# The hand-written order at the mixer/FFN boundary carried on through the squares of x1; the last norm weight loaded into the place of the up projection's activations

## The chip, the cores and the metric

One core of one Trainium2 chip runs the kernel. The metric is the device time of one execution in microseconds (us), as the median of several runs; a profile is one further execution with its own time.

## What is computed

One decoder layer for 256 tokens of width 2048, all in float32. Cut to what matters here:

```python
x = x + rms_norm(mixed, ln_mix_post)          # mixed = [attention || SSM] @ w_out
h = rms_norm(x, ln_ffn_pre)                   # this x is called x1 below
u = causal_depthwise_conv(h @ w_ffn_up, ffn_conv_w, ffn_conv_b)
gate, up = split(u, [5632])
f = (gelu(gate) * up) @ w_ffn_down
x = x + rms_norm(f, ln_ffn_post)
# rms_norm(x, w) = x * rsqrt(mean(x*x) + 1e-6) * w
```

## The kernel before

**Weights.** Every matrix is read in units of 128 x 1024 float32 (512 KB). SyncE issues the load of a unit into one of 4 `raw` buffers (L71). ScalarE rounds it to float32r, `whi` (L72), VectorE takes the rest, `wlo = raw - whi` (L73), and TensorE multiplies with both. A load can start when the `wlo` of four units before is done, and a cast when TensorE is through with the unit whose `whi` place it takes. From the boundary on there are 4 + 3 places for `whi` and for `wlo` (`ws.deepen`). A unit of the up projection is 8 pairs of products (L202 with `whi`, L203 with `wlo`); a unit of the down projection is 12 products (L265 to L267). `fetch` loads and splits one unit; `fetch_rounded` only loads and casts it and hands back the subtraction for later. `tick` fetches one unit (two, while the deeper buffers fill) and counts down the work that `defer(n, ...)` put off by n units.

**The boundary.** The last chunk of `w_out` ends in an order written by hand for TensorE, ScalarE and VectorE (`tc.manual_schedule`); elsewhere a scheduler orders each engine's instructions. In the written part the two token halves (t = 0, 1) get the factor of the norm behind the mixer (`factor`), x1 times the next norm's weight is formed in four chunks of 512 columns (`scaled`), transposed on TensorE (`turn`, L785), and evacuated as a high part by ScalarE (L787) and a low part by VectorE (`finish`, L790) into `h2`, the activations of the up projection. Three column tiles of the up projection (`held_up`, six units) are multiplied token half by token half as the pieces come (L210, L213).

The rms factor of this second norm is not in `h2`. It is multiplied in later, behind the up projection, by `rb2`, which holds it along tokens. For this, x1 itself is formed in `xt` (`residual`, L778 on VectorE, 8 pieces of which one is done early), each piece is squared and summed on ScalarE (L185, output `junk`), and `second_rms` reduces the sums on VectorE (`sum1`), takes the power on GpSimd (`rsy`, L144) and refines it on VectorE (`rsq`, then `rsr`, L148). Two TensorE transposes (`prb`, L179) and a ScalarE copy (L180) bring it into `rb2`. They are deferred by 5 units:

```python
defer(5, lambda: along_tokens(rb2, [sums[:, t:t + 1] for t in range(NT)]))
defer(60, load_post)
```

**The last norm weight.** `wpo` holds `ln_ffn_post` on all partitions. `load_post` (deferred by 60 units) issues a broadcast load of 1024 KB from GpSimd's queue and multiplies the tile by -0.5 on ScalarE. It is first read when the first column chunk of the second half of the down projection is complete (`fdone`, L939). The FFN runs in two halves: 22 pairs of column tiles of the up projection with convolution and gelu (`gated`) into `gT`, then four chunks of the down projection.

Of the kernel before, what the change touches and what calls it, by code (L numbers as in the profile page):

```python
# [9 lines left out]
F32 = mybir.dt.float32  # L10
# [9 lines left out]
P = 128  # L20
D = 2048
S = 256
NT = S // P
# [23 lines left out]
V_MIXPOST, V_FFNPRE, V_FFNPOST, V_HEADS = 0, D, 2 * D, 3 * D  # L47
# [68 lines left out]
def decoder_layer(ctx, tc, x, xT, win, wdt, wout, wup, wdown, relb, vec, cols, mconv, fconv,  # L116
                  consts, onehot, out):
    nc = tc.nc
    ctx.enter_context(nc.allow_non_contiguous_dma(reason="overlapping rows of the bias table"))

    pers = ctx.enter_context(tc.tile_pool(name="pers", bufs=1))
# [4 lines left out]
    aux = nc.gpsimd.dma_start  # L126

    def row_bcast(off, n):
        return bass.AP(tensor=vec.tensor, offset=vec.offset + off, ap=[[0, P], [1, n]])
# [7 lines left out]
    def chunk(c):  # L137
        return slice(c * 512, (c + 1) * 512)
# [12 lines left out]
    def mean_rsqrt(src, inv):  # L151

        w = src.shape[-1]
        a = pers.tile([P, w], F32, name="rsa", tag=f"rsa{w}", bufs=4)
        nc.vector.tensor_scalar(a, src, inv, EPS, op0=ALU.mult, op1=ALU.add)
        return rsqrt(a)
# [27 lines left out]
    def square_sum(dst, src):  # L184
        nc.scalar.activation(junk, src, AF.Square, accum_out=dst)  # L185
# [37 lines left out]
    def defer(units, fn, *args):  # L223

        pending.append([units, fn, args])

    def tick():
        ws.tick()
        for p in pending:
            p[0] -= 1  # L230
        due = [p for p in pending if p[0] <= 0]
        pending[:] = [p for p in pending if p[0] > 0]
        for _, fn, args in due:
            with tc.issue_after(end[0]):
                fn(*args)
# [56 lines left out]
    def rows_tail(pss, aT, kts, tail, t, j):  # L292
        rows_part(pss[t], tail[j], aT, kts[len(kts) - HOLD + j], t, False, j == HOLD - 1)

    ws = Weights(nc, wp, [win[i] for i in range(win.shape[0])]
                 + [wout[i] for i in range(wout.shape[0])]
                 + [w for half in range(2)
                    for w in [wup[half * 88 + i] for i in range(88)]
                    + [wdown[half * 44 + i] for i in range(44)]])
# [19 lines left out]
    with ExitStack() as mctx:  # L319
# [404 lines left out]
        xt = pers.tile([P, NT, D], F32, name="xt", tag="xt", bufs=1)  # L724
# [16 lines left out]
        ss1 = pers.tile([P, NT, 4], F32, name="ss1")  # L741
# [18 lines left out]
        def factor(t, ps):  # L760

            square_sum(ss[0][t][:, 3:4], ps)
            return late_rsqrt(ss[0][t][:, 3:4], early[t], lambda: nc.vector.tensor_tensor(
                mm[:, t, chunk(3)], ps, wpost[:, chunk(3)], op=ALU.mult))

        def scaled(t, q):

            if (t, q) == (0, 3):
                residual(t, q)
                nc.vector.tensor_tensor(ml[t][q], xt[:, t, chunk(q)], lnrow[:, chunk(q)],  # L770
                                        op=ALU.mult)
            else:
                nc.vector.scalar_tensor_tensor(ml[t][q], ml[t][q], rs[t], xl[t][q], op0=ALU.mult,
                                               op1=ALU.add)

        def residual(t, q):
            x1 = xt[:, t, chunk(q)]
            nc.vector.scalar_tensor_tensor(x1, mm[:, t, chunk(q)], rs[t], x1, op0=ALU.mult,  # L778
                                           op1=ALU.add)

        def turned(t, q):
# [8 lines left out]
                last.append(nc.vector.tensor_tensor(dst[1], pt, f32(dst[0]), op=ALU.subtract).ins)  # L790
            return rest, last

        def second_rms():
            for t in range(NT):
                for q in range(4):
                    if (t, q) != (0, 3):
                        residual(t, q)
                    square_sum(ss1[:, t, q:q + 1], xt[:, t, chunk(q)])
            a = pers.tile([P, NT], F32, name="sum1")
            nc.vector.tensor_reduce(a, ss1, axis=AX.X, op=ALU.add)  # L800
            return mean_rsqrt(a, 1.0 / D)
# [13 lines left out]
        rs, rest, units = [], {}, []  # L815
# [6 lines left out]
        def second_tokens(q):  # L822
            for i, ps in enumerate(held_up):
                for k in range(q * 4, q * 4 + 4):
                    cols_tok(ps, units[k // 8 * 3 + i], h2, k, k % 8, 1)
# [5 lines left out]
        def turn(t, q):  # L831
            rest[t, q] = turned(t, q)

        def finish(t, q):
            rest[t, q][0]()

        E = mybir.EngineType
        with tc.manual_schedule(engines={E.PE, E.Activation, E.DVE}):
            for j in range(HOLD):
                rows_tail(pss, mT, both, tail, 0, j)  # L840
            rs.append(factor(0, pss[0]))
            scaled(0, 0)
            scaled(0, 1)
            scaled(0, 2)
            t1_units(0, 1)
            more = [ws.fetch_rounded()]
            t1_units(1, 2)
            more.append(ws.fetch_rounded())
            t1_units(2, 3)
            turn(0, 0)  # L850
            turn(0, 1)
            finish(0, 0)
            finish(0, 1)
            scaled(0, 3)
            more[0]()
            t1_units(3, 4)
            more.append(ws.fetch_rounded())
            t1_units(4, 5)
            rs.append(factor(1, pss[1]))
            more.append(ws.fetch_rounded())  # L860
            units.extend(ws.take() for _ in range(6))
            turn(0, 2)
            first_tokens(0)
            turn(0, 3)
            scaled(1, 0)
            finish(0, 2)
            first_tokens(1)
            scaled(1, 1)
            finish(0, 3)
            turn(1, 0)  # L870
            first_tokens(2)
            turn(1, 1)
            finish(1, 0)
            more[1]()
            finish(1, 1)
            first_tokens(3)
            scaled(1, 2)
            weighted(1, 3)
            second_tokens(0)
            turn(1, 2)  # L880
            scaled(1, 3)
            more[2]()
            finish(1, 2)
            more[3]()
            second_tokens(1)
            turn(1, 3)
            finish(1, 3)
            second_tokens(2)
            second_tokens(3)
        tick()  # L890
        came = rest[1, 3][1]
        with tc.issue_after(came[0]), tc.issue_after(came[1]):
            for _ in range(5):
                tick()
            sums = second_rms()

    fp = ctx.enter_context(tc.tile_pool(name="fp", bufs=1))
    fcv = fp.tile([P, 2 * NF, 4], F32, name="fcv")
    aux(out=fcv, in_=fconv)
    wpo = fp.tile([P, D], F32, name="wpo")  # L900
    gT = fp.tile([P, HALF, 2, S], F32R, name="gT")
    fa = pers.tile([P, NT, D], F32, name="fa", tag="mm", bufs=1)
    rb2 = pers.tile([P, S], F32, name="rb2", tag="rbc", bufs=1)

    def load_post():
        aux(out=wpo, in_=row_bcast(V_FFNPOST, D))
        nc.scalar.mul(wpo, wpo, -0.5)

    def summed(ps):
        u = fp.tile([P, S], F32, name="cfu", tag="cf", bufs=8)  # L910
# [52 lines left out]
    def gated(i, ug, uu):  # L963
        cg = conv_ffn(i, ug)
        nc.scalar.activation(cg, cg, AF.Gelu_apprx_tanh)
        cu = conv_ffn(NF + i, uu)
        k = i % HALF
        nc.vector.tensor_tensor(cu, cg, cu, op=ALU.mult)
        split_evac(gT, k, slice(0, S), cu)

    held = []
    defer(5, lambda: along_tokens(rb2, [sums[:, t:t + 1] for t in range(NT)]))
    defer(60, load_post)
    for half in range(2):
        for i in range(half * HALF, (half + 1) * HALF):
            ps = held_up[2 * i:2 * i + 2]
            for _ in range(2 - len(ps)):
                ps.append(col_psum())
                cols_tile(ps[-1], h2)
            us = [summed(p) for p in ps]  # L980
            if i < 2:
                defer(5 - 2 * i, gated, i, *us)
            else:
                gated(i, *us)
        for c in range(4):
            if half == 0 and c >= 2:
                held.append([psum("ph") for _ in range(NT)])
                rows_chunk(held[-1], gT, range(0, HALF, 2), last=False)
            elif half == 1 and c == 2:
                rows_chunk(held[0], gT, range(0, HALF, 2), first=False, done=fdone(1, c))  # L990
            elif half == 1 and c == 3:
                fearly += [early_sum(ss[2][t][:, :3]) for t in range(NT)]
                kts = range(0, HALF, 2)
                tail = rows_to_tail(held[1], gT, kts, first=False)
                for t in range(NT):
                    for j in range(HOLD):
                        rows_tail(held[1], gT, kts, tail, t, j)
                    fdone(1, 3)(t, held[1][t])
            else:
                rows_chunk(chunk_psums(), gT, range(0, HALF, 2), done=fdone(half, c))  # L1000
# [105 lines left out]
```

## Time and profile before

| | |
|---|---|
| median of 3 runs | 1142.55 us (1141.38 to 1145.75) |
| the profiled execution | 1141.79 us |
| its span from first to last instruction | 1140.0 us |
| TensorE busy (products) | 1126.8 us, 99% |
| VectorE / ScalarE / GpSimd busy | 788.4 / 592.2 / 12.0 us |
| mean granted TensorE clock | 0.997 of full |

A time in a row below is counted from the start of the span. PE is TensorE, PEld its weight loads, DVE VectorE, ACT ScalarE, POOL GpSimd, SP SyncE; a q behind the name (SPq) is the engine's issue of DMAs. In a timeline a row holds start, duration, engine, line, operation, output<-input, shapes and count, and in brackets how long the engine stood idle before it and what released it.

### The profile page before, as it was taken

Reading aid. Unit: us, or ns where it says so; the run is one execution under the profiler, and the core shown is the slowest. Engines: PE = TensorE matmul, PEld = TensorE weight load, DVE = VectorE, ACT = ScalarE, POOL = GpSimd, SP = SyncE. Lnnn points to the kernel's source line nnn. Section 1 sums busy time; section 2 is a strip of 40 time slices with the busy share of each in tenths; the row PEclk is TensorE's granted clock in tenths of the full one; section 3 lists DMA queues with packets and bytes.
Section 4 is the critical chain, followed back from the end, with each engine's and each line's share of the span. In section 5 each row is a group of like instructions: output and inputs, shape, how many; then the busy total and the mean of one; then the engine's idle time right before and its main releaser. Section 6 shows DMA issues by size and latency. Waiting matters only on the chain.

```text
span 1140.0 us, 15818 instructions
## 1 busy us (share of the span) xinstructions
PE 1126.8 (99%) x5912; PEld 957.3 (84%) x5912; DVE 788.4 (69%) x1268; ACT 592.2 (52%) x913; POOL 12.0 (1%) x22
## 2 busy tenths in 40 slices
PE   9999999999999989999999999999999999999997
PEld 7877888888878978888888888888888888888886
DVE  6587886766667788787877644447878777765552
ACT  6555544554454476555555544335555555554441
POOL 0000000000000000000000000000000000000000
PEclk9999999999999999999999999999999999999999
DMA  8756444555587275565556565566555555655542
GB/s 299 285 169 197 141 158 135 183 169 167 173 328 242 97 272 173 192 189 186 185 186 186 188 196 186 187 194 189 187 185 186 186 187 190 191 188 186 188 161 74
DMA packets 60148, 215.53 MB, mean 189 GB/s; under 512 B 7119, under 2 KB 7800, under 8 KB 59176
## 3 DMA queue, kind: packets, MB, share of 16 engines
q1 hardware_dynamic: 58696, 207.69, 56.3%
q0 software_dynamic: 1088, 6.48, 1.6%
q8 instruction: 46, 0.75, 0.3%
q10 hardware_dynamic: 288, 0.35, 0.1%
q14 instruction: 30, 0.25, 0.1%
HBM read 212.39 MB, written 2.11 MB: 188 GB/s over the span
## 4 chain that ended last, share of the span: by engine, by line
PE 94%; DMA 2%; ACT 1%; DVE 1%; issue 1%; SPq 0%; POOL 0%; POOLq 0%; ACTq 0%
PE pa L202 35%; PE pa L203 18%; PE pa L265 8%; PE pa L266 8%; PE pa L267 8%; PE ph L267 4%; PE ph L266 4%; PE ph L265 4%; PE pab L202 1%; DMA raw<-in_wout_dram 1%; DMA wpo<-in_vec_dram 1%; DVE wlo L73 1%; PE py L568 1%; PE pab L203 1%; ACT whi L72 1%
## 5 line engine op out<-in xcount | busy, mean ns | idle before, releaser
L73 DVE TENSOR_TENSOR wlo<-raw,whi 128x1024 fp32r<-128x1024 f32 (+1 forms) x385 | 469.5, 1222 | 271.1 <-ACT whi L72 262.0
L72 ACT CAST whi<-raw 128x1024 fp32r<-128x1024 f32 (+1 forms) x385 | 402.8, 1047 | 466.1 <-PE pa L202 221.5
L202 PE MATMUL pa<-h,whi 128*128 128x512 f32 x1360 | 479.7, 396 | 0.0
L203 PE MATMUL pa<-h,wlo 128*128 128x256 f32 x1360 | 384.1, 282 | 0.0
L202 PEld LDWEIGHTS pa<-h,whi 128*128 128x128 f32 x1360 | 256.2, 188 | 60.3
L203 PEld LDWEIGHTS pa<-h,wlo 128*128 128x128 f32 x1360 | 256.5, 189 | 0.1
L202 PE MATMUL pa<-hT,whi 128*128 128x512 f32 x384 | 138.5, 399 | 0.0
L203 PE MATMUL pa<-hT,wlo 128*128 128x256 f32 x384 | 108.3, 283 | 0.0
L202 PEld LDWEIGHTS pa<-hT,whi 128*128 128x128 f32 x384 | 72.2, 188 | 16.5 <-issue 0.2
L920 DVE SCALAR_TENSOR_TENSOR cfc<-cfu,fcv,cfc 128x254 f32<-128x254 f32 (+1 forms) x176 | 83.4, 479 | 1.9 <-ACT cfc L918 0.5
L203 PEld LDWEIGHTS pa<-hT,wlo 128*128 128x128 f32 x384 | 72.2, 188 | 0.3 <-issue 0.2
L267 PE MATMUL pa<-whi,gT 128*128 128x512 f32 x176 | 69.4, 394 | 0.0
L267 PE MATMUL ph<-whi,gT 128*128 128x512 f32 x176 | 69.3, 394 | 0.0
L265 PE MATMUL ph<-whi,gT 128*128 128x512 f32 x176 | 69.2, 393 | 0.0
L266 PE MATMUL ph<-wlo,gT 128*128 128x512 f32 x176 | 69.2, 393 | 0.0
L265 PE MATMUL pa<-whi,gT 128*128 128x512 f32 x176 | 69.2, 393 | 0.0
L266 PE MATMUL pa<-wlo,gT 128*128 128x512 f32 x176 | 69.2, 393 | 0.0
L918 ACT ACTIVATE cfc<-cfu,fcv 128x256 f32<-128x256 f32 x88 | 52.3, 599 | 0.6 <-DVE cfu L917 0.6
L265 PE MATMUL pa<-whi,hT 128*128 128x512 f32 x128 | 51.7, 404 | 0.2 <-DVE xsT L219 0.2
L267 PE MATMUL pa<-whi,hT 128*128 128x512 f32 x128 | 50.7, 396 | 0.0
L266 PE MATMUL pa<-wlo,hT 128*128 128x512 f32 x128 | 50.6, 395 | 0.0
L266 PE MATMUL pa<-wlo,mT 128*128 128x512 f32 x128 | 50.2, 392 | 0.3 <-DVE wlo L73 0.3
(238 smaller groups left out, 1148.1 us busy)
## 6 DMA issues: line engine op xcount, KB each, us to landing
raw<-in_wup_dram SPq DMA_DIRECT2D x176, 512.0 KB, 3.6
raw<-in_wdown_dram SPq DMA_DIRECT2D x88, 512.0 KB, 3.5
raw<-in_win_dram SPq DMA_DIRECT2D x87, 512.0 KB, 3.5
raw<-in_wout_dram SPq DMA_DIRECT2D x32, 512.0 KB, 4.2
xsq<-in_x_dram SPq DMA_DIRECT2D x2, 1024.0 KB, 8.0
xt<-in_x_dram POOLq DMA_DIRECT2D x2, 1024.0 KB, 7.0
xr<-in_xT_dram SPq DMA_DIRECT2D x7, 256.0 KB, 6.1
out_dram<-xt SPq DMA_DIRECT2D x6, 256.0 KB, 2.4
```

Of the source, the lines that this page charges most:

```text
L72: nc.scalar.copy(hi[:, s], raw[:, s])
L73: return lambda: nc.vector.tensor_tensor(lo[:, s], raw[:, s], f32(hi[:, s]), op=ALU.subtract)
L202: nc.tensor.matmul(ps, w[0][:, s], aT[:, k, :, :], start=(k == 0), stop=False)
L203: end[0] = nc.tensor.matmul(ps[:, :S], w[1][:, s], aT[:, k, 0, :], start=False, stop=(k == KT - 1)).ins
L265: nc.tensor.matmul(ps, a, w[0][:, s], start=(first and j == 0), stop=False)
L266: nc.tensor.matmul(ps, a, w[1][:, s], start=False, stop=False)
L267: end[0] = nc.tensor.matmul(ps, b, w[0][:, s], start=False, stop=(last and j == 1)).ins
L568: nc.tensor.matmul(py[:, i * 64:(i + 1) * 64], rows[:, t, g, i, :], xcs[t, g][:, i * 64:(i + 1) * 64], start=True, stop=True)
L918: nc.scalar.activation(c, u, AF.Identity, scale=wv[:, 2:3], bias=wv[:, 3:4])
L920: nc.vector.scalar_tensor_tensor(c[:, sh:], u[:, :S - sh], wv[:, 2 - sh:3 - sh], c[:, sh:], op0=ALU.mult, op1=ALU.add)
```

## The change

Two things are edited. First, the written order does not stop behind the last `second_tokens`: the pieces of x1, their squares and four more units of weights (`more[4]` to `more[7]`) are written into it piece by piece, with the square of the chunk that is done early (0, 3) first. The scheduler's part behind it fetches two units instead of six before the sums are reduced. Second, `wpo` no longer has a place of its own. It is allocated behind the up projection of the second half under the tag of `h2`, and loaded and scaled there.

```diff
+        def second_square(t, q):
+            square_sum(ss1[:, t, q:q + 1], xt[:, t, chunk(q)])
+
         def second_rms():
-            for t in range(NT):
-                for q in range(4):
-                    if (t, q) != (0, 3):
-                        residual(t, q)
-                    square_sum(ss1[:, t, q:q + 1], xt[:, t, chunk(q)])
             a = pers.tile([P, NT], F32, name="sum1")
             nc.vector.tensor_reduce(a, ss1, axis=AX.X, op=ALU.add)
             return mean_rsqrt(a, 1.0 / D)
@@ -878,33 +876,44 @@
             weighted(1, 3)
             second_tokens(0)
             turn(1, 2)
+            more.append(ws.fetch_rounded())
             scaled(1, 3)
+            finish(1, 2)
             more[2]()
-            finish(1, 2)
             more[3]()
             second_tokens(1)
             turn(1, 3)
             finish(1, 3)
+            more[4]()
             second_tokens(2)
             second_tokens(3)
-        tick()
-        came = rest[1, 3][1]
-        with tc.issue_after(came[0]), tc.issue_after(came[1]):
-            for _ in range(5):
-                tick()
-            sums = second_rms()
+            second_square(0, 3)
+            more.append(ws.fetch_rounded())
+            for q in range(2):
+                residual(0, q)
+                second_square(0, q)
+            more[5]()
+            more.append(ws.fetch_rounded())
+            residual(0, 2)
+            second_square(0, 2)
+            residual(1, 0)
+            second_square(1, 0)
+            more[6]()
+            more.append(ws.fetch_rounded())
+            for q in range(1, 4):
+                residual(1, q)
+                second_square(1, q)
+            more[7]()
+        for _ in range(2):
+            tick()
+        sums = second_rms()
 
     fp = ctx.enter_context(tc.tile_pool(name="fp", bufs=1))
     fcv = fp.tile([P, 2 * NF, 4], F32, name="fcv")
     aux(out=fcv, in_=fconv)
-    wpo = fp.tile([P, D], F32, name="wpo")
     gT = fp.tile([P, HALF, 2, S], F32R, name="gT")
     fa = pers.tile([P, NT, D], F32, name="fa", tag="mm", bufs=1)
     rb2 = pers.tile([P, S], F32, name="rb2", tag="rbc", bufs=1)
-
-    def load_post():
-        aux(out=wpo, in_=row_bcast(V_FFNPOST, D))
-        nc.scalar.mul(wpo, wpo, -0.5)
 
     def summed(ps):
         u = fp.tile([P, S], F32, name="cfu", tag="cf", bufs=8)
@@ -970,7 +979,6 @@
 
     held = []
     defer(5, lambda: along_tokens(rb2, [sums[:, t:t + 1] for t in range(NT)]))
-    defer(60, load_post)
     for half in range(2):
         for i in range(half * HALF, (half + 1) * HALF):
             ps = held_up[2 * i:2 * i + 2]
@@ -982,6 +990,10 @@
                 defer(5 - 2 * i, gated, i, *us)
             else:
                 gated(i, *us)
+        if half == 1:
+            wpo = pers.tile([P, D], F32, name="wpo", tag="h", bufs=1)
+            aux(out=wpo, in_=row_bcast(V_FFNPOST, D))
+            nc.scalar.mul(wpo, wpo, -0.5)
         for c in range(4):
             if half == 0 and c >= 2:
                 held.append([psum("ph") for _ in range(NT)])
```

**The squares on ScalarE.** The first rows are ScalarE's before, from the scaling of `wpo` on, with the second to the sixth of the eight squares (`junk,ss1_3090<-xt`); whi is a unit's cast, cfu the copy of a finished column tile out of PSUM.

```order
L907 ACTIVATE wpo_3879<-wpo_3879 128x2048
L72 CAST whi_3840<-raw_3839 128x1024
L185 ACTIVATE junk_67,ss1_3090<-xt_3066 128x512
L72 CAST whi_3907<-raw_3906 128x1024
L185 ACTIVATE junk_67,ss1_3090<-xt_3066 128x512
L72 CAST whi_3929<-raw_3928 128x1024
L185 ACTIVATE junk_67,ss1_3090<-xt_3066 128x512
L218 COPY cfu_3934<-pq_3491 128x256
L185 ACTIVATE junk_67,ss1_3090<-xt_3066 128x512
L218 COPY cfu_3937<-pa_3889 128x256
L185 ACTIVATE junk_67,ss1_3090<-xt_3066 128x512
```

The same stretch of ScalarE with the change, from the third square to the cast behind the eighth and last:

```order
L185 ACTIVATE junk_67,ss1_3090<-xt_3066 128x512
L72 CAST whi_3826<-raw_3825 128x1024
L185 ACTIVATE junk_67,ss1_3090<-xt_3066 128x512
L218 COPY cfu_3885<-pa_3490 128x256
L185 ACTIVATE junk_67,ss1_3090<-xt_3066 128x512
L72 CAST whi_3836<-raw_3835 128x1024
L185 ACTIVATE junk_67,ss1_3090<-xt_3066 128x512
L72 CAST whi_3849<-raw_3848 128x1024
L185 ACTIVATE junk_67,ss1_3090<-xt_3066 128x512
L72 CAST whi_3855<-raw_3854 128x1024
L185 ACTIVATE junk_67,ss1_3090<-xt_3066 128x512
L72 CAST whi_3906<-raw_3905 128x1024
```

The scaling of `wpo` is gone from here; a cast and a square or two alternate up to the last square, and the cast of the seventh unit (`whi_3906`) comes behind it. The six units that TensorE takes next are whi_3726, 3816, 3826, 3836, 3849 and 3855 (before: 3810, 3816, 3822, 3828, 3834, 3840).

**The norm's factor on VectorE.** VectorE's rows before, which end with the factor `rsr`:

```order
L73 TENSOR_TENSOR wlo_3930<-raw_3928,whi_3929 128x1024
L219 TENSOR_TENSOR cfu_3934<-pq_3491,cfu_3934 128x256
L219 TENSOR_TENSOR cfu_3937<-pa_3889,cfu_3937 128x256
L73 TENSOR_TENSOR wlo_3959<-raw_3957,whi_3958 128x1024
L73 TENSOR_TENSOR wlo_3981<-raw_3979,whi_3980 128x1024
L800 TENSOR_REDUCE sum1_3860<-ss1_3090 128x2
L155 TENSOR_SCALAR rsa_3862<-sum1_3860 128x2
L145 TENSOR_TENSOR rsq_3865<-rsy_3864 128x2
L73 TENSOR_TENSOR wlo_4004<-raw_4002,whi_4003 128x1024
L146 TENSOR_TENSOR rsq_3865<-rsq_3865,rsa_3862 128x2
L147 TENSOR_SCALAR rsq_3865<-rsq_3865 128x2
L148 TENSOR_TENSOR rsr_3866<-rsy_3864,rsq_3865 128x2
```

With the change:

```order
L73 TENSOR_TENSOR wlo_3856<-raw_3854,whi_3855 128x1024
L798 TENSOR_REDUCE sum1_3860<-ss1_3090 128x2
L219 TENSOR_TENSOR cfu_3882<-pa_3489,cfu_3882 128x256
L155 TENSOR_SCALAR rsa_3862<-sum1_3860 128x2
L219 TENSOR_TENSOR cfu_3885<-pa_3490,cfu_3885 128x256
L145 TENSOR_TENSOR rsq_3865<-rsy_3864 128x2
L73 TENSOR_TENSOR wlo_3907<-raw_3905,whi_3906 128x1024
L146 TENSOR_TENSOR rsq_3865<-rsq_3865,rsa_3862 128x2
L219 TENSOR_TENSOR cfu_3933<-pq_3491,cfu_3933 128x256
L147 TENSOR_SCALAR rsq_3865<-rsq_3865 128x2
L73 TENSOR_TENSOR wlo_3929<-raw_3927,whi_3928 128x1024
L148 TENSOR_TENSOR rsr_3866<-rsy_3864,rsq_3865 128x2
```

Before, three subtractions `wlo` for later units stood ahead of the reduction `sum1` in these rows and one inside the chain; now the reduction comes right behind the sixth unit's `wlo_3856`, and two subtractions (3907, 3929) and three of the sums `cfu` stand between the steps of the chain. On TensorE `prb` has moved up by one pair of products: it stood behind the first pair of the sixth unit (`whi_3840`), now it stands right ahead of that unit (`whi_3855`).

**The scaling of wpo on ScalarE.** ScalarE's rows before at the start of the second half's down projection, where `cfc` and `gT` belong to the last column tiles of the up projection and the whi are units of `w_ffn_down`:

```order
L72 CAST whi_9431<-raw_9430 128x1024
L965 ACTIVATE cfc_9384<-cfc_9384 128x256
L918 ACTIVATE cfc_9390<-cfu_9381,fcv_3877 128x256
L72 CAST whi_9449<-raw_9448 128x1024
L190 CAST gT_3880<-cfc_9390 128x256
L72 CAST whi_9467<-raw_9466 128x1024
```

And with the change:

```order
L72 CAST whi_9431<-raw_9430 128x1024
L974 ACTIVATE cfc_9381<-cfc_9381 128x256
L927 ACTIVATE cfc_9387<-cfu_9378,fcv_3877 128x256
L996 ACTIVATE wpo_9395<-wpo_9395 128x2048
L190 CAST gT_3879<-cfc_9387 128x256
L72 CAST whi_9449<-raw_9448 128x1024
L72 CAST whi_9467<-raw_9466 128x1024
```

The scaling of `wpo`, which waits for its load, now stands ahead of the last `gT` and of all casts of the down projection from `whi_9449` on. On GpSimd's queue the load waits for TensorE's last product with `h2`, and stands behind the power `rsy` instead of ahead of it.

## Rows read from the trace of the kernel before

**Rows 1.** The page: the span, and the busy time of the engines.
```profile
span 1140.0 us, 15818 instructions
...
PE 1126.8 (99%) x5912; PEld 957.3 (84%) x5912; DVE 788.4 (69%) x1268; ACT 592.2 (52%) x913; POOL 12.0 (1%) x22
```

**Rows 2.** Waits on TensorE, whole span: total us, times, longest.
```profile
PE prb L179 <- DVE rsr L148: 4.5, 1, 4.5
```

**Rows 3.** Two stretches: span, busy time by engine, granted clock, DMA share, GB/s.
```profile
402.90:417.30 14.40, 14.40 (x84) 12.47 (x82) 11.07 (x15) 11.73 (x22) 0.00 (x0) 1.00 0.76 279
422.20:426.20 4.00, 4.00 (x16) 3.40 (x15) 4.00 (x10) 2.45 (x5) 0.00 (x0) 0.57 0.77 244
```

**Rows 4.** Timeline of TensorE, from the second tokens to behind the gap.
```profile
399.25 0.28 PE L213 MATMUL pq<-h,wlo 128*128 128x256 f32 x1
...
402.89 0.39 PE L202 MATMUL pa<-h,whi 128*128 128x512 f32 x1
...
416.97 0.39 PE L202 MATMUL pa<-h,whi 128*128 128x512 f32 x1
...
421.99 0.43 PE L179 MATMUL prb<-cst,rsr 128*128 128x128 f32 x2 [4.51 <-DVE rsr L148]
422.17 0.48 PE L202 MATMUL pa<-h,whi 128*128 128x512 f32 x1
...
426.25 0.40 PE L202 MATMUL pa<-h,whi 128*128 128x512 f32 x1
```

**Rows 5.** Timeline of ScalarE around the squares of x1.
```profile
397.46 0.59 ACT L787 CAST h<-pxt 128x512 fp32r<-128x512 f32 x1 [2.62 <-PE pxt L785]
...
404.85 1.05 ACT L72 CAST whi<-raw 128x1024 fp32r<-128x1024 f32 x1 [3.08 <-DMA raw<-in_wup_dram]
...
406.89 1.92 ACT L907 ACTIVATE wpo<-wpo 128x2048 f32<-128x2048 f32 x1 [0.72 <-DMA wpo<-in_vec_dram]
...
409.65 0.62 ACT L185 ACTIVATE junk<-xt 128x512 f32<-128x512 f32 x1
...
410.27 1.03 ACT L72 CAST whi<-raw 128x1024 fp32r<-128x1024 f32 x1
```

**Rows 6.** Timeline of VectorE around the same stretch.
```profile
394.88 0.69 DVE L790 TENSOR_TENSOR h<-pxt,h 128x512 fp32r<-128x512 f32 x1 [0.69 <-ACT h L787]
...
399.35 3.49 DVE L73 TENSOR_TENSOR wlo<-raw,whi 128x1024 fp32r<-128x1024 f32 x3
...
407.07 2.73 DVE L778 SCALAR_TENSOR_TENSOR xt<-mm,lsr,xt 128x512 f32<-128x512 f32 x4
...
412.25 0.75 DVE L219 TENSOR_TENSOR cfu<-pa,cfu 128x256 f32<-128x256 f32 x2
...
419.12 0.17 DVE L155 TENSOR_SCALAR rsa<-sum 128x2 f32<-128x2 f32 x1
...
420.13 0.16 DVE L145 TENSOR_TENSOR rsq<-rsy 128x2 f32<-128x2 f32 x1 [0.84 <-POOL rsy L144]
```

**Rows 7.** DMA issues of three stretches: KB each, median us from issue to landing.
```profile
wpo<-in_vec_dram POOLq DMA_DIRECT2D x1, 1024.0 KB, 8.3
raw<-in_wup_dram SPq DMA_DIRECT2D x1, 512.0 KB, 7.4
...
raw<-in_wup_dram SPq DMA_DIRECT2D x1, 512.0 KB, 4.6
...
lnrow<-in_vec_dram POOLq DMA_DIRECT2D x1, 1024.0 KB, 15.2
```

**Rows 8.** Timeline of ScalarE at the start of the second down projection.
```profile
1015.10 1.05 ACT L72 CAST whi<-raw 128x1024 fp32r<-128x1024 f32 x1 [0.88 <-PE pa L267]
...
1017.89 1.05 ACT L72 CAST whi<-raw 128x1024 fp32r<-128x1024 f32 x1 [1.44 <-PE pa L267]
```

**Rows 9.** TensorE's last product with h2, and VectorE's first reading of wpo.
```profile
1009.25 0.28 PE L203 MATMUL pa<-h,wlo 128*128 128x256 f32 x1
...
1042.31 1.29 DVE L939 TENSOR_TENSOR fa<-fa,wpo 128x512 f32<-128x512 f32 x2
```

## The prediction, as put on record before the run

> **What bounds the kernel now.** I read the page first. TensorE is busy for 1126.8 of 1140.0 us [rows 1]: only time in which TensorE stands still, or runs slowly, can be won. The waits on TensorE come second. By far the longest is 4.5 us, once, of `prb` for the factor `rsr` [rows 2]. The windows around it show a second cost: up to 417.3 TensorE is busy throughout at a granted clock of 1.00, and in the 4.0 us behind the gap the clock is 0.57 [rows 3], a mixture of its two levels, 2.4 and 1.2 GHz; ahead of it the engine had stood still.
>
> The full price is read from TensorE's timeline. From 402.89 to 416.97 it starts 40 pairs of products, 0.352 us a pair [rows 4]. The pair at 416.97 is the first of the sixth unit; without a gap its second would start at 417.32. Seven pairs and the two transposes remain up to the seventh unit: 417.32 + 7 x 0.352 + 0.18 (from the start of `prb` to the next product, 421.99 to 422.17) = 419.96. It starts at 426.25 [rows 4]. So the wait costs **6.3 us**: 4.67 of standing still (421.99 - 417.32) and 1.6 of slow products behind it.
>
> Why is `rsr` late? The sums of the squares are through the first step only at 419.12 [rows 6]. Two things had held ScalarE up before the squares. A cast waited 3.08 us for its raw unit, up to 404.85, and then the scaling of `wpo` waited 0.72 and took 1.92 [rows 5]. Both go back to one transfer: `wpo`'s 1024 KB took 8.3 us (so they were issued near 398.6), and a raw unit issued beside them took 7.4 where one issued as they ended took 4.6 [rows 7].
>
> **The change part by part.** *Nothing is added or dropped.* The same products, casts, squares, loads and sums run; so the sum consists of waits alone.
>
> *1. The squares.* I follow the new order with the durations of the rows. In VectorE's queue a subtraction takes 1.16 (3.49 / 3), a piece of x1 0.68 (2.73 / 4), a sum `cfu` 0.37 (0.75 / 2); on ScalarE a cast takes about 0.95 to 1.05 and a square with its readout 0.62 (409.65 to 410.27) [rows 5, 6]. Up to VectorE's evacuation at 394.88 the two orders are alike. Then VectorE: `wlo_3590` to 396.7, `wlo_3611` to 397.8, the last evacuation from 398.08 (ScalarE's part ends at 398.05 [rows 5]) to 398.7, `wlo_3727` to 399.8, two pieces of x1 to 401.2, `wlo_3817` to 402.3, two pieces to 403.7, `wlo_3827` to 404.8, three pieces to 406.8, then 3837 to 408.0, 3850 to 409.1 and 3856 to 410.3. ScalarE runs beside it and is free from 398.05: square, cast 3816 to 399.6, second square at 400.5, and so on; its eighth square can end at 409.5, ahead of VectorE, if the raw units come in time. Each raw unit is issued when a subtraction four units before ends. Cast 3826 starts at 402.3 and its unit is issued at 396.8; 3836: 404.8 and 397.9; 3849: 406.3 and 399.9; 3855: 407.9 and 402.4. That leaves 5.5, 6.9, 6.4 and 5.5 us. With 4.6 us for a unit nothing waits; with 7.4 each would.
>
> The factor then: reduction 410.3, a `cfu`, `rsa` from 410.8, the step through GpSimd (419.12 to 420.13, 1.01 [rows 6]) to 411.8, `wlo_3907` to 413.1, `rsq` and a `cfu` to 413.8, `wlo_3929` to 415.0, `rsr` to **415.2**. `wlo_3929` needs cast 3928, whose unit is issued at 408.0: with 4.6 us it lands at 412.6 and is cast by 413.7, in time. TensorE comes to `prb` at 416.97, since it now stands ahead of the sixth unit. So there are about 1.8 us to spare, the wait disappears whole, the engine does not stand still and the clock stays up: -6.3 us. Which landing time I take decides: 4.6, because what made 7.4 is the 1024 KB transfer that is no longer there; 7.4 is the bad bound, costed as a rival. What is late next, if anything, is a subtraction: `wlo_3590` now comes behind an evacuation instead of ahead of it, and so 3590 and 3611 end at 396.7 and 397.8. TensorE wants 3611 in the product at 399.25 [rows 4] and 3590 eight products earlier: 1.4 us of room. All later units are ready 3 to 10 us ahead. I cost these moves at nothing; if the cover went, each us late costs a us and, by the gap above, up to 1.6 more in clock.
>
> *2. The load of `wpo`.* It is now issued when TensorE has read `h2` for the last time, 1009.5 in the times of before (1009.25 + 0.28) [rows 9]. With 8.3 us [rows 7] it lands at 1017.8, and ScalarE, which waits for it from 1014.2 on (free since 0.88 before 1015.10 [rows 8]), has scaled it by 1019.8 (1.92). Queued behind it on ScalarE are the last `gT` and every cast of the down projection; behind those casts wait VectorE's subtractions, the raw loads and at last TensorE. The cast at 1015.10 is the first that is held up. It fills one of seven places, just left by TensorE, so it is used six units later; TensorE frees one each 2.79 us [rows 8], so about 1031.8. With 0.40 for `gT`, 1.05 for the cast and 1.22 for the subtraction ScalarE must be through with `wpo` by 1029.1: 9.3 us of room. The casts behind it run at 1.05 each against 2.79 of need and catch up. The slowest broadcast load of this size in the trace, `lnrow` with 15.2 us [rows 7], would still leave 2.4 us. `gT` is read in the eleventh unit, and `wpo` at 1042.31 [rows 9]. So: 0 from both ends; the load costs from 17.6 us on.
>
> The Trainium skill (DMA: Bandwidth & Descriptors, Rules for kernel authors) speaks against this part: issue a load early, compute, and wait for it late, while here the wait stands right behind the issue. By that rule ScalarE pays most of the load, and the rows agree that it would stand idle for some 3.6 us; but by the room just worked out none of it reaches TensorE, and the sum is the same.
>
> **The sum.** 1141.79 (span 1140.0 and 1.79 around it) - 6.3 = 1135.5 for an execution like the profiled one. The profiled one lies 0.76 under the median of the runs, by which it would be 1136.3. I say **1135.9**. A difference of 0.5%, 5.7 us, is about what can be told from no change here; the bound is 1136.8, and my forecast is only just past it.
>
> **The rivals.** *Part of the wait stays.* If raw units keep taking 7.4 us, I get cast 3826 at 404.2, 3855 at 409.9, the reduction at 412.1, cast 3928 at 417 and `rsr` at 419.6 in place of 415.2. TensorE then waits 2.6 and the clock may fall again, up to 1.6: 1137.6 to 1139.7, say 1138.5. For it speaks that six raw units are now asked for between 402 and 411, at a DMA share already at 0.76 [rows 3]; against it, that the 1024 KB are gone.
>
> *It doesn't do what it says:* the written order delays the second tokens' products by more than the 1.4 us of room, and a wait there takes the place of the one removed. TensorE would stop around 398 with the same fall of the clock; about 1141.5. Against it: the evacuations it hangs on are at the same places as before.
>
> *Slower: the load of `wpo` starves the down projection.* A load issued by GpSimd is held up while VectorE is busy, ScalarE waits on, and the seven places run dry. It costs from 17.6 us of landing time, undoes the gain at 23.9, and is slower by 0.5% from 29.6; at twice `lnrow`'s time, 30.4 us, 1135.5 + 12.8 = 1148.3. Against it: the 8.3 us were measured while VectorE ran three subtractions without a pause [rows 6, 7], and the down projection uses VectorE less. The Trainium skill has a rule that would make this happen (SBUF — State Buffer, SBUF: two separate sides): certain two-port VectorE instructions lock GpSimd out, so that it can't write its descriptors. No row here shows such a hold-up.
>
> **Chances and range.** The wait gone whole 0.78, part of it 0.12, no gain 0.06, slower 0.04. In the first case the forecast passes the 0.5% bound by 0.5 to 1.3 us, and the three runs shown spread over 4.4 us, so I count some 0.72 of it as faster: 0.57 in all. Within 0.5%: 0.22 + 0.12 + 0.04 = 0.38. Slower: 0.05, with a little for what I don't see. The range is 1134.2 (the lowest run, 1141.38, less 6.3, and 0.9 below that) to 1139.3, which takes in most of the second case.
>
> **What the new profile would show.** Right: no wait of `prb` for `rsr`, a clock of 1.00 in the stretch around 417 to 427, `rsr` at 415 or 416, a span near 1133.7; ScalarE idle for 3 to 4 us ahead of the scaling of `wpo` near 1008 to 1014, and TensorE without a gap in the 30 us behind. Wrong: a wait on TensorE of more than 1 us between 390 and 430, or in the second down projection; raw units landing in 7 us between 400 and 410; or a time that hasn't moved although the wait is gone, which would mean that another limit, such as the feeding of units, takes the time back later.

## The result, and the profile after

The changed kernel takes **1135.01 us** (median of 4 runs, 1134.70 to 1135.06), the kernel before 1142.64 beside it (4 runs, 1141.38 to 1145.75): a ratio of **0.9935**, 95% interval 0.9923 to 0.9948. The profiled execution took 1135.06.

The page of the changed kernel, which answers to [rows 1]:

```profile
span 1133.3 us, 15814 instructions
...
PE 1124.5 (99%) x5912; PEld 955.2 (84%) x5912; DVE 787.2 (69%) x1268; ACT 591.8 (52%) x913; POOL 12.1 (1%) x22
```

The span is 6.7 us shorter. TensorE itself is busy for 2.3 us less with the same 5912 products, so part of the gain is products that ran faster. All waits on TensorE (us in total, times, longest):

```profile
PE pa L963 <- ACT diag L961: 1.6, 1, 1.6
PE pab L202 <- ACT whi L72: 1.4, 2, 1.2
PE idle L316 <- DVE zero L313: 1.1, 1, 1.1
PE pa L265 <- DVE xsT L219: 0.2, 1, 0.2
```

The wait of `prb` for `rsr` [rows 2] is gone, and nothing near the boundary or in the second down projection stands in its place. Two stretches around the place where it stood, with the busy time of PE, PEld, DVE, ACT and POOL, the granted clock, the DMA share and GB/s:

```profile
402.90:417.00 14.10, 14.10 (x83) 12.31 (x82) 13.35 (x22) 10.68 (x21) 0.72 (x1) 1.00 0.74 249
417.00:427.00 10.00, 10.00 (x59) 8.79 (x58) 8.33 (x19) 8.56 (x14) 0.00 (x0) 1.00 0.54 184
```

The second stretch takes in what was the gap and the four slow microseconds behind it [rows 3]: now 59 products without a pause at a clock of 1.00. TensorE's timeline at `prb` and at the last product with `h2`, which answers to [rows 4, 9]:

```profile
416.48 0.38 PE L179 MATMUL prb<-cst,rsr 128*128 128x128 f32 x2
416.61 0.48 PE L202 MATMUL pa<-h,whi 128*128 128x512 f32 x1
...
1002.53 0.28 PE L203 MATMUL pa<-h,wlo 128*128 128x256 f32 x1
```

`prb` has no bracket: the engine did not stand idle before it. Why `rsr` came in time is read on ScalarE and VectorE, against [rows 5, 6]. ScalarE:

```profile
393.76 0.59 ACT L787 CAST h<-pxt 128x512 fp32r<-128x512 f32 x1 [4.05 <-PE pxt L785]
...
397.45 0.63 ACT L185 ACTIVATE junk<-xt 128x512 f32<-128x512 f32 x1
...
407.28 1.04 ACT L72 CAST whi<-raw 128x1024 fp32r<-128x1024 f32 x1
408.22 0.63 ACT L185 ACTIVATE junk<-xt 128x512 f32<-128x512 f32 x1
408.75 0.19 ACT L185 ACTIVATION_READ_ACCUMULATOR junk<-xt 128x1 f32 x1
...
413.46 1.05 ACT L72 CAST whi<-raw 128x1024 fp32r<-128x1024 f32 x1 [1.41 <-DMA raw<-in_wup_dram]
```

VectorE:

```profile
394.38 0.69 DVE L790 TENSOR_TENSOR h<-pxt,h 128x512 fp32r<-128x512 f32 x1 [1.81 <-ACT h L787]
394.99 2.35 DVE L73 TENSOR_TENSOR wlo<-raw,whi 128x1024 fp32r<-128x1024 f32 x2
...
409.64 0.16 DVE L798 TENSOR_REDUCE sum<-ss 128x2 f32<-128x8 f32 x1
...
411.05 0.16 DVE L145 TENSOR_TENSOR rsq<-rsy 128x2 f32<-128x2 f32 x1 [0.52 <-POOL rsy L144]
...
413.90 0.16 DVE L148 TENSOR_TENSOR rsr<-rsy,rsq 128x2 f32<-128x2 f32 x1
```

The first square now runs as soon as ScalarE's last evacuation is through, the eighth ends at 408.94, and `rsr` is done at 414.06, 2.4 us before TensorE comes to `prb`. Casts do wait for raw units (1.41 at 413.46), but only behind the squares. The DMA issues, of 396.5 to 402.6 and of 1000 to 1012 (KB each, median us to landing), against [rows 7]:

```profile
raw<-in_wup_dram SPq DMA_DIRECT2D x4, 512.0 KB, 4.6
...
wpo<-in_vec_dram POOLq DMA_DIRECT2D x1, 1024.0 KB, 6.2
```

And ScalarE at the second down projection, which answers to [rows 8]; GpSimd issued the load at 1003.37:

```profile
1005.60 1.05 ACT L72 CAST whi<-raw 128x1024 fp32r<-128x1024 f32 x1 [1.05 <-PE pa L267]
...
1009.59 1.92 ACT L996 ACTIVATE wpo<-wpo 128x2048 f32<-128x2048 f32 x1 [2.09 <-DMA wpo<-in_vec_dram]
1011.40 0.39 ACT L190 CAST gT<-cfc 128x256 fp32r<-128x256 f32 x1
1011.70 1.99 ACT L72 CAST whi<-raw 128x1024 fp32r<-128x1024 f32 x2
1013.96 1.05 ACT L72 CAST whi<-raw 128x1024 fp32r<-128x1024 f32 x1 [0.27 <-PE pa L267]
1016.75 1.05 ACT L72 CAST whi<-raw 128x1024 fp32r<-128x1024 f32 x1 [1.74 <-PE pa L267]
```

ScalarE stands idle for `wpo`, makes up two casts, and from 1013.96 on waits for TensorE again: the delay never reached it.

### The profile page after: what moved, and what is told of

Its sections match the earlier page's. It is cut to its first block, busy times and chain, and to the rows that moved or that the text cites. A ratio compares the mean times of both kernels' runs of the same rounds, so it can differ in the third digit from the quotient of the medians.

```text
span 1133.3 us, 15814 instructions
## 1 busy us (share of the span) xinstructions
PE 1124.5 (99%) x5912; PEld 955.2 (84%) x5912; DVE 787.2 (69%) x1268; ACT 591.8 (52%) x913; POOL 12.1 (1%) x22
## 4 chain that ended last, share of the span: by engine, by line
PE 98%; DMA 0%; DVE 0%; ACT 0%; issue 0%; SPq 0%; POOLq 0%; ACTq 0%
PE pa L202 36%; PE pa L203 18%; PE pa L265 9%; PE pa L266 9%; PE pa L267 9%; PE ph L267 4%; PE ph L265 4%; PE ph L266 4%; PE pab L202 1%; PE pa L210 1%; PE py L568 1%; PE pab L203 1%; DMA raw<-in_win_dram 0%; PE pq L210 0%; PE pa L213 0%; PE pxt L785 0%
## 5 line engine op out<-in xcount | busy, mean ns | idle before, releaser
L265 PE MATMUL pa<-whi,mT 128*128 128x512 f32 x128 | 50.5, 394 | 0.0
```

Source lines behind the costliest of these rows:

```text
L265: nc.tensor.matmul(ps, a, w[0][:, s], start=(first and j == 0), stop=False)
```

## The experiments

The first four ran beside ten runs of the kernel before (median 1142.08, 1140.58 to 1143.21), the last four beside fifteen (1142.23, 1139.65 to 1143.58).

| kernel | median us (lowest to highest) | ratio to before, 95% |
|---|---|---|
| order alone | 1135.09 (1134.47 to 1135.29) | 0.9938 [0.9924, 0.9952] |
| load of `wpo` alone | 1138.49 (1137.31 to 1139.06) | 0.9969 [0.9957, 0.9980] |
| `prb` one unit later | 1138.69 (1136.99 to 1139.37) | 0.9969 [0.9956, 0.9981] |
| `wpo` loaded four times | 1135.19 (1134.79 to 1135.78) | 0.9941 [0.9928, 0.9953] |
| `prb` two units earlier | 1135.79 (1135.38 to 1136.16) | 0.9940 [0.9928, 0.9953] |
| scaling held, one load | 1134.72 (1134.58 to 1135.48) | 0.9933 [0.9920, 0.9945] |
| scaling held, two loads | 1135.47 (1135.27 to 1136.13) | 0.9939 [0.9925, 0.9952] |
| scaling held, three loads | 1141.81 (1140.77 to 1145.06) | 1.0001 [0.9991, 1.0011] |

### The order alone

The changed kernel with `wpo` back in its own place and at its old time:

```diff
+    wpo = fp.tile([P, D], F32, name="wpo")
...
+    defer(60, load_post)
...
-        if half == 1:
-            wpo = pers.tile([P, D], F32, name="wpo", tag="h", bufs=1)
-            aux(out=wpo, in_=row_bcast(V_FFNPOST, D))
-            nc.scalar.mul(wpo, wpo, -0.5)
```

> The changed kernel with the load and scaling of the last norm weight put back to where they were (own place, deferred by 60 units); only the written order is new. My theory (the factor came late, and its whole wait was the cost): the scaling now stands behind the eighth square on ScalarE, so it no longer delays the squares; the transfer still slows raw units from about 4.6 to 7.4 us, which moves the factor by 1 to 2 us, from 414.1 in the changed kernel to 415 or 416, still ahead of the 416.5 at which TensorE asks for it. So a wait of 0 to 1 us and 1135 to 1136.5 us. Rival (the transfer is the cause, the order does nothing): the factor late by 3 us or more, 1139 to 1142 us.

It brings the whole gain. The raw units issued from 396.5 to 402.6, beside `wpo`'s transfer (8.0 us), again took long:

```profile
raw<-in_wup_dram SPq DMA_DIRECT2D x4, 512.0 KB, 6.2
```

Yet on ScalarE one cast ahead of the last squares waited, and the scaling came behind the squares, not ahead of them:

```profile
407.12 1.05 ACT L72 CAST whi<-raw 128x1024 fp32r<-128x1024 f32 x1 [1.08 <-DMA raw<-in_wup_dram]
...
411.72 1.92 ACT L921 ACTIVATE wpo<-wpo 128x2048 f32<-128x2048 f32 x1
```

VectorE made the reduction at 410.90 and `rsr` at 414.36:

```profile
414.36 0.15 DVE L148 TENSOR_TENSOR rsr<-rsy,rsq 128x2 f32<-128x2 f32 x1
```

That is 0.5 later than in the changed kernel, where 1 to 2 were expected; 0.2 of it was there before the squares (393.99 against 393.76 at the evacuation L787). TensorE came to `prb` at 416.70 without a pause.

### The load of wpo alone

The kernel before with only `wpo` moved:

```diff
-    wpo = fp.tile([P, D], F32, name="wpo")
...
-    defer(60, load_post)
...
+        if half == 1:
+            wpo = pers.tile([P, D], F32, name="wpo", tag="h", bufs=1)
+            aux(out=wpo, in_=row_bcast(V_FFNPOST, D))
+            nc.scalar.mul(wpo, wpo, -0.5)
```

> The kernel before with only the last norm weight moved behind the up projection; the order at the boundary stays the scheduler's. My theory: ScalarE is free of the 3.08 us wait for a raw unit and of 2.64 us for the scaling, but three casts still stand between the squares and three subtractions ahead of the reduction; worked out with the rows of before the factor is ready near 419.5, against 417.2 when it is wanted. A wait of 1 to 3 us, and a clock that falls for part of the time behind it: 1137.5 to 1140 us. Rival (the transfer is the whole cause): no wait, 1135 to 1136 us. Rival (the order is the whole cause): 1141 to 1143 us.

About half of the gain. Its raw units of 396.5 to 402.6 landed in 4.8 us, the cast that had waited 3.08 [rows 5] waited 1.86, the scaling was out of the way, and `rsr` came at 418.70. What is left of the wait on TensorE, and the stretch around it:

```profile
PE prb L179 <- DVE rsr L148: 2.0, 1, 2.0
...
416.50:427.00 10.50, 8.46 (x50) 7.19 (x49) 9.44 (x24) 7.79 (x14) 0.72 (x1) 1.00 0.60 218
```

The gap is 2.04 us and the clock behind it stayed at 1.00 in this execution, the fastest of the six (1137.31; the others took 1138.03 to 1139.06). The last product with `h2`:

```profile
1004.77 0.28 PE L203 MATMUL pa<-h,wlo 128*128 128x256 f32 x1
```

It starts 2.24 behind the changed kernel's, with the same start at the boundary (393.76): the gap and little more.

### The reader of the factor one unit later

The kernel before, its squares, its order and its load left as they are; only the two transposes and what hangs on them are deferred by one more unit:

```diff
-    defer(5, lambda: along_tokens(rb2, [sums[:, t:t + 1] for t in range(NT)]))
+    defer(6, lambda: along_tokens(rb2, [sums[:, t:t + 1] for t in range(NT)]))
...
-                defer(5 - 2 * i, gated, i, *us)
+                defer(6 - 2 * i, gated, i, *us)
```

> The kernel before with the two transposes of the factor, and the first two gated pairs that need it, deferred by 6 units instead of 5; nothing else is touched. My theory (only the wait on TensorE counts, and everything around it is hidden): TensorE asks at about 420.0 for a factor that is ready at 421.9, so it waits 1.9 us instead of 4.5; with the clock's share still to pay 1139 to 1140 us, without it 1138 us or less. Rival (the gain comes from ScalarE and VectorE being fed in a better order, not from the wait): no change, 1142 us.

`rsr` is as late as before (421.88), but is wanted later:

```profile
PE prb L179 <- DVE rsr L148: 2.9, 1, 2.9
...
416.50:427.00 10.50, 7.58 (x37) 6.41 (x36) 9.13 (x18) 7.36 (x14) 0.72 (x1) 0.84 0.86 273
```

The wait was 2.92 and not the 1.9 expected, since TensorE asked at 419.18 and not at 420.0. Even so it is 1.6 shorter than before, the span 2.4 and the median 3.4, with nothing done sooner behind the boundary: the price lies in TensorE's stop, not in late casts or squares as such. Of the span's 2.4, 0.73 was there at the evacuation L787 (393.52; 394.25 in the trace of before), and 1.7, about the 1.6, is left. Here the clock did fall (0.84). The evacuation and the last product with `h2`:

```profile
393.52 0.59 ACT L787 CAST h<-pxt 128x512 fp32r<-128x512 f32 x1 [4.05 <-PE pxt L785]
...
1006.85 0.28 PE L203 MATMUL pa<-h,wlo 128*128 128x256 f32 x1
```

The product starts 4.32 behind the changed kernel's; this execution was 0.24 ahead of it at the evacuation (393.52 against 393.76), so the stop cost 4.56: 2.92 of standing still and 1.6 of slow products.

### wpo loaded four times

```diff
-            aux(out=wpo, in_=row_bcast(V_FFNPOST, D))
+            for _ in range(4):
+                aux(out=wpo, in_=row_bcast(V_FFNPOST, D))
```

> The changed kernel with the last norm weight loaded four times into the same place, one load behind the other, ahead of its scaling; it tests the room that was worked out for that load (17.6 us from issue to landing before TensorE is late). One load takes 6.2 us there; beside 217 GB/s of raw units I expect four to be through after 18 to 22 us. My theory: the scaling ends 1 to 4 us too late and TensorE waits about as long at the seventh unit of the second down projection: 1135.5 to 1140 us, and no wait at all if they land within 17.6 us. Rival (ScalarE's standing idle costs from the first us on): 12 us or more, 1147 us.

GpSimd waited for each load before it issued the next, and ScalarE had `wpo` 31 us after the first issue; still there is no wait on TensorE. But this was no test of the room. ScalarE's timeline:

```profile
1008.52 1.05 ACT L72 CAST whi<-raw 128x1024 fp32r<-128x1024 f32 x1 [0.88 <-PE pa L267]
...
1022.40 1.05 ACT L72 CAST whi<-raw 128x1024 fp32r<-128x1024 f32 x1 [1.70 <-PE pa L267]
1034.61 1.92 ACT L997 ACTIVATE wpo<-wpo 128x2048 f32<-128x2048 f32 x1 [11.17 <-DMA wpo<-in_vec_dram]
1036.43 3.88 ACT L72 CAST whi<-raw 128x1024 fp32r<-128x1024 f32 x4
```

The scheduler that orders this stretch had put the scaling six casts further back, behind the cast at 1022.40. The first cast held up would have run near 1025.2; by the prediction's way of counting ScalarE then had until 1039.6 (16.7 us for six units, less 1.05 and 1.22), and it was through at 1036.5. So the next kernels hold the scaling in its place.

### The scaling held in its place: one, two and three loads

Every cast that the next chunk of the down projection fetches is queued behind the scaling, and `wpo` is loaded once, twice or three times (here three):

```diff
-            aux(out=wpo, in_=row_bcast(V_FFNPOST, D))
-            nc.scalar.mul(wpo, wpo, -0.5)
+            for _ in range(3):
+                aux(out=wpo, in_=row_bcast(V_FFNPOST, D))
+            pin = nc.scalar.mul(wpo, wpo, -0.5).ins
...
+                if half == 1 and c == 0:
+                    with tc.issue_after(pin):
+                        rows_chunk(chunk_psums(), gT, range(0, HALF, 2), done=fdone(half, c))
```

> The changed kernel with ScalarE's place of the scaling held: every cast of the first unit row of the second down projection stands behind it, so the first cast held up is the one at 1002.9 in the run that loaded wpo four times, and not that at 1011.7. Theory (the seven places of cast units are the room): that cast is used 16.7 us later, at 1019.5; with 1.05 for the cast and 1.22 for the subtraction ScalarE must be through with wpo by 1017.2. One load issued at 1003.4 lands by 1011.5 at the latest and is scaled by 1013.4: no wait on TensorE, time 1135.1, ratio 0.994. Rival (holding casts back costs as such): waits of pa for wlo from 1010 on, over 1138.

> As the run with the scaling held in its place, and wpo is loaded twice, the second load behind the first (GpSimd waits for the first to land). By the run with four loads the second lands near 1019.4, so the scaling ends at 1021.3, 4.1 us behind the limit of 1017.2. Theory (the seven places are the room): TensorE waits about 4.1 us for a subtraction near 1019, and the clock may fall behind it: 1139.2 to 1140.8, ratio 0.9975 to 0.999. Rival (the room is wider than the seven places, or the load is hidden anyway, as with four loads): no wait, 1135.2, ratio 0.994.

> As before, with three loads in a row. By the run with four loads the third lands near 1027.1 and is scaled by 1029.1, 11.9 us behind the limit of 1017.2. Theory: TensorE waits about 11.9 us near 1019, with up to 1.6 us of slow clock behind: 1147.0 to 1148.6, ratio 1.0045 to 1.006, so the change would have been slower than the kernel before. Rival (the room is wider, or the load is hidden anyway): 1135.2, ratio 0.994.

One load: scaled from 1009.98 to 1011.90, then four casts back to back; no wait on TensorE, and the time of the changed kernel. Two loads, ScalarE and then TensorE:

```profile
1016.30 1.92 ACT L997 ACTIVATE wpo<-wpo 128x2048 f32<-128x2048 f32 x1 [9.18 <-DMA wpo<-in_vec_dram]
1018.12 3.88 ACT L72 CAST whi<-raw 128x1024 fp32r<-128x1024 f32 x4
...
1020.46 0.50 PE L266 MATMUL pa<-wlo,gT 128*128 128x512 f32 x1 [0.59 <-DVE wlo L73]
```

Three loads:

```profile
1020.15 1.91 ACT L997 ACTIVATE wpo<-wpo 128x2048 f32<-128x2048 f32 x1 [13.29 <-DMA wpo<-in_vec_dram]
1021.96 3.88 ACT L72 CAST whi<-raw 128x1024 fp32r<-128x1024 f32 x4
...
1023.04 0.73 PE L265 MATMUL pa<-whi,gT 128*128 128x512 f32 x2 [3.65 <-ACT whi L72]
1024.30 0.80 PE L266 MATMUL pa<-wlo,gT 128*128 128x512 f32 x1 [0.53 <-DVE wlo L73]
...
1019.00:1032.00 13.00, 8.82 (x32) 6.57 (x31) 6.30 (x6) 8.04 (x8) 0.00 (x0) 0.87 0.51 176
```

The mechanism is the expected one; the sizes are not, since the loads landed sooner (7.4 and 5.0 us, and 6.1, 5.1 and 5.1) than in the run with four (7.6 at the median), so ScalarE was through at 1018.1 and 1022.0 and not at 1021.3 and 1029.1. Measured against those times the limit holds: with two loads TensorE was late by 0.59, so the limit lies at 1018.12 - 0.59 = 1017.5 (expected 1017.2); with three, 1021.96 - 1017.5 = 4.5 of lateness stand against 3.65 + 0.53 = 4.2 of waits. With three the span is 6.4 over that with one: 0.3 was there already when the load was issued (1003.29 against 1003.00), 4.2 are the waits, and the remaining 1.9 go with the slow clock (0.87 in the stretch). That uses up the whole gain of the change: at 1.0001 the kernel is as slow as before. By its time alone (1135.47 against 1134.72) the run with two loads could hardly be told from the rival, in which there is no wait; the trace and the run with three loads decide.

### The reader two units earlier

The changed kernel, with

```diff
-    defer(5, lambda: along_tokens(rb2, [sums[:, t:t + 1] for t in range(NT)]))
+    defer(3, lambda: along_tokens(rb2, [sums[:, t:t + 1] for t in range(NT)]))
```

> The changed kernel with the broadcast products of rsr two units' places earlier: in the profile of the changed kernel TensorE would come to that place at 413.4 to 413.5, and rsr is written at 414.06. Theory (a stop costs its own length, and the clock falls behind a longer one only, as the 2.04 us without a fall and the 2.92 and 4.51 us with one have shown so far): a wait of 0.6 to 0.7 us, a clock of 1.00 behind it, time 1135.7, ratio 0.994. Rival (every stop at this place lets the clock fall): the same wait and 1.6 us of slow products behind it, time 1137.3, ratio 0.9955, granted clock 0.85 or less in 414:425.

```profile
PE prb L179 <- DVE rsr L148: 0.5, 1, 0.5
...
412.00:427.00 15.00, 14.48 (x84) 12.47 (x84) 14.16 (x30) 12.72 (x20) 0.00 (x0) 1.00 0.74 257
```

A gap of 0.5 and a clock of 1.00: as the theory has it, a short stop costs about its length (1135.79, 0.7 or 0.8 over the changed kernel and the order alone, across the two sets of runs).

## Why the prediction was right

**The price of the wait** (predicted 6.3). From the start of the span to the last product with `h2` the changed kernel is 6.72 ahead (1002.53 against 1009.25 [rows 9]). The evacuation on ScalarE that comes ahead of every edit (L787) was already 0.49 earlier (393.76); in the trace of before it is this row:

```profile
394.25 0.59 ACT L787 CAST h<-pxt 128x512 fp32r<-128x512 f32 x1 [4.05 <-PE pxt L785]
```

That is variation from run to run: in the first three of the experiments it starts at 393.52 to 393.99. 6.72 - 0.49 = 6.23. The split into standing still and slow clock is borne out by the kernels that keep one and not the other: a stop of 2.04 at full clock cost 2.2, stops of 2.92 and 4.2 with a fall of the clock cost 4.6 and 6.1.

**The cause.** That `wpo`'s transfer lengthens the raw loads is shown: 6.9, 6.2 and 7.5 us at the median where it runs beside them (before, order alone, `prb` one unit later), 4.6 and 4.8 where it does not (changed, load alone). That it is *the* cause is too much. Taking it away alone leaves 2.04 us of wait; leaving it there in the new order leaves none. The written order puts the squares ahead of casts and of the scaling in ScalarE's queue. It also puts the pieces of x1 that they read ahead of subtractions in VectorE's queue, which the prediction's answer to why `rsr` is late leaves out. Before, six of the seven pieces that were left stood behind a subtraction that waited for the late cast, and the first four of them ran from 407.07 on [rows 6]; in the changed kernel the first two of the seven run from 399.33 on. VectorE before, that subtraction and the reduction:

```profile
405.93 1.23 DVE L73 TENSOR_TENSOR wlo<-raw,whi 128x1024 fp32r<-128x1024 f32 x1 [3.09 <-ACT whi L72]
...
418.93 0.15 DVE L800 TENSOR_REDUCE sum<-ss 128x2 f32<-128x8 f32 x1
```

VectorE in the changed kernel, the first two pieces:

```profile
399.33 1.41 DVE L778 SCALAR_TENSOR_TENSOR xt<-mm,lsr,xt 128x512 f32<-128x512 f32 x2
```

No run changes one of the two queues alone. The reduction's own place was not what made it late: it starts 0.6 us behind the end of the eighth square before (418.38) and 0.7 behind it in the changed kernel (408.94).

**The new order.** The queue was followed closely. With the 0.49 taken off, the eighth square was to end at 409.0 and ended at 408.94, the reduction to start at 409.8 and started at 409.64, `rsr` to be ready at 414.7 and was at 414.06: from the start of the reduction on the chain took 4.4 us where 4.9 were added up, a little less at each step. 2.4 us were to spare where 1.8 were said. The 1.4 us of room for the two moved subtractions held: they end at 397.3, and TensorE has no wait there.

**The landing time that was to decide** is the weakest step: "Which landing time I take decides: 4.6". In the order alone the four units landed in 3.6, 6.3, 7.4 and 6.2 us, against the leads of 5.5, 6.9, 6.4 and 5.5 that the prediction lists. The third fell short by 1.0, and its cast waited 1.08; the fourth's shortfall was hidden behind that wait. `rsr` came 0.5 later, and 2.2 us were still to spare (414.36 + 0.15 to 416.70). The rival with 7.4 us for every unit did not come about, so whether it would have kept 2.6 us of wait stays open.

**The load of wpo** (predicted 0, costs from 17.6 us of landing). It landed in 6.2 in place of 8.3, ScalarE waited 2.1 in place of 3.6, and TensorE did not wait. The room is borne out too. ScalarE had to be through by 1029.1 less the 6.72 gained, 1022.4, and was through at 1011.4: 11.0 us to spare. That is the 9.3 said plus the 2.1 by which the load was faster, less about 0.5: the load was issued 0.6 behind the end of the last product with `h2` (1002.81 to 1003.37), where the prediction has no gap. That the limit is where this way of counting puts it is what the two and three loads show, in an order whose limit lies earlier (1017.5). Loading early instead, as the rule of the Trainium skill cited in the prediction has it (DMA: Bandwidth & Descriptors, Rules for kernel authors: issue early, wait late), is the order alone, and it gives the same time, 1135.09. The rival in which VectorE holds up GpSimd's loads and the second down projection starves did not come about: there `wpo` landed in 5.0 to 8.1 us in all of these kernels, and in 6.2 in the changed one with VectorE busy for 74% of the time (1003 to 1010). The rule that the prediction names for it (the Trainium skill, SBUF — State Buffer, SBUF: two separate sides) is about two-port VectorE instructions, which lock GpSimd out. No run here shows whether any of VectorE's instructions beside these loads is one, so the rule itself stays untested.

**The sum.** 1135.5 for an execution like the profiled one against 1135.06, the difference being about the run-to-run 0.49. The forecast for the median, 1135.9, came out 0.9 too high. By medians the gain is 7.6 in the first comparison and 7.0 between the order alone and the ten runs beside it. The 1.3 over my 6.3 has two parts: 0.85 that the median of the four runs before stood above the profiled execution (1142.64 against 1141.79), and the 0.49. So the 6.3 is the price in one execution; how far it differs in others is taken up in the last section.

## What to carry to other kernels

Price a wait on the bounding engine from the timeline up to the point where its old rhythm is back, not by the length of the gap alone: here the slow products behind added a third in the profiled execution. Then ask what stands ahead of the late result in its engine's queue, since putting the few small instructions that it needs first brought the whole gain with the slow transfer still in place. A load that is waited for right behind its issue was free here as long as the buffers behind it outlasted it; count that room in places times the consumer's rhythm, and test it with the order pinned, because a scheduler may quietly move the wait, as it did with four loads.

## What the runs showed of the hardware that was not expected

**The clock fell behind some stops and not behind others.** TensorE stood still for 0.5, 0.6 and 2.04 us and went on at a granted clock of 1.00; it stood for 2.92, for 3.65 and shortly after 0.53, and for 4.51 us, and the products behind ran at a lower clock (0.84, 0.87 and 0.83 to 0.84 over the 10 to 13 us stretches around them), at a price of 1.6 to 1.9 us. Each is one profiled execution, that of the 2.04 us the fastest of its six runs and that of the 2.92 us the slowest of its five. So it is not shown that the length of the stop decides.

**Kernels with a long stop vary more.** Lowest to highest run lie 1.8 to 4.4 us apart in the kernels with a stop of 2 us or more, and 0.4 to 1.0 in those without. The mean granted clock that is on record for each run fits a share of slow clock that differs from run to run. Of the 25 runs of the kernel before that ran beside the experiments, the 11 with a mean clock of 0.997 or 0.998 took 1141.2 us on average, and the 14 with 0.995 or 0.996 took 1142.7. With `prb` one unit later, the three runs at 0.999 took 1136.99 to 1138.69 and the two at 0.998 took 1139.14 and 1139.37. With the load of `wpo` alone, the fastest run has 0.998 and four of the other five 0.997, so the clock may have fallen behind that stop as well; the fifth, 1138.19 at 0.999, does not fit. Where in a run the slow stretch lies is seen only in the profiled ones, and why it comes in some runs and not in others stays open.

**The same 1024 KB load took 5.0 to 8.1 us in the second down projection.** It was shortest, 5.0 and 5.1, for the second of two loads and the second and third of three, when the held-up casts had stopped the issue of raw loads. It took 6.1 to 8.1 where raw units were issued shortly before it or beside it. VectorE stood still during the short ones too, so the traces do not show by themselves which of the two mattered; but the fourth of four loads took 7.4, and VectorE stood still then as well.
